# A recurrence's ScalarE and VectorE steps given an issue time 12 nominal microseconds ahead of their TensorE visit

## The chip, the cores and the metric

One Trainium2 chip, one of its cores. The metric is the device time of one execution in microseconds (us), as the median of several runs. TensorE, VectorE, ScalarE, GpSimd and SyncE each work through a list of instructions of their own, in order; semaphores hold an instruction until what it needs has been written.

In the rows of the profile PE is TensorE's matmuls, PEld its weight loads, DVE VectorE, ACT ScalarE, POOL GpSimd and SP SyncE.

## What is computed

A decoder layer with two kinds of heads side by side, on 1024 tokens of width 2048 in float32. One projection feeds an RWKV-7 mixer (16 heads of 64) and a sliding-window attention (16 query heads); a second projection brings both back. Cut to what matters here:

```python
h = rms_norm(x, norm_w)
z = h @ w_in                                   # 2048 x 6528
y_rwkv = rwkv7_mixer(z[..., :RWKV_COLS], ...)  # per head: a 64 x 64 state, one step per token
y_att  = swa_sink_mixer(z[..., RWKV_COLS:], ...)
return x + concatenate([y_rwkv, y_att]) @ w_out

def step(state, inp):                          # inside rwkv7_mixer
    r_t, w_t, k_t, v_t, kk_t, a_t = inp
    sa = einsum('bhvk,bhk->bhv', state, -kk_t)
    state = (state * w_t[:, :, None, :] + sa[..., None] * (kk_t * a_t)[:, :, None, :]
             + v_t[..., None] * k_t[:, :, None, :])
    return state, einsum('bhvk,bhk->bhv', state, r_t)
```

## The kernel before

**Tiling.** The 1024 tokens go through in two halves of 512. In each half there are eight units, u0 to u7 in the first and u8 to u15 in the second; a unit is a pair of RWKV heads together with a pair of attention heads. A unit computes six z tiles of 128 channels by 512 tokens. Each z tile is 48 matmuls of 128 x 512: the input and the weights are both split in a high and a low part, and three of the four products are taken (L346, L347 and L351). Each weight block is split by a ScalarE cast (L321) and a GpSimd subtraction (L322). After the eight units of each half comes the output projection (L798 to L800).

**The recurrence.** It doesn't go token by token. `rwkv_prep` rewrites 64 tokens (a chunk) as small matrices, and `rwkv_chain` carries the state through the 8 chunks c0 to c7 of a unit. Chunk c needs from its state `svu[:, :, c, :]`:

1. TensorE, L596: O = F x state, two small matmuls, one for each head.
2. ScalarE, L599: s0 = state scaled by the decay `pe`, two halves of 64 x 64; then L601 copies O over the state, again two halves.
3. TensorE, L603: ch = k x (that copy), and L604, which adds to O.
4. VectorE, L607: next state = ch x pe + s0, two halves; for c7 it goes to `scar`, the state kept for the other half of the tokens. The two halves are called the pair of the chunk here.

L596 of chunk c+1 needs the pair of chunk c. So a unit's chain is eight round trips TensorE, ScalarE, TensorE, VectorE, with no step of which another step of the same unit can run.

**What sets the order.** All work is written as generators that yield a nominal time; `run` takes the one with the earliest time, and `at(t)` gives what is then issued the priority `100000 + int(t * 1000)`. Every engine's list is made from these priorities and from what depends on what. A z matmul counts 0.32 nominal us, a z tile 15.36. The chain's chunk c is due at `tc0 = t0 + 91.5 + 5c`; its L603 and what follows at `tc0 + 2.5`.

What stands beside the chain of a unit in the lists, with its lines: on TensorE the z matmuls of the next unit, the attention's scores (L701, L702) and small products for the next unit's preparation (L398, L399, L573, L574); on VectorE the attention's score bias (L714), its maximum (L716, L718) and its normalising (L724, L725, L727) and the next unit's sigmoid, whose last step is a reciprocal of 128 x 512 (L410, L411); on ScalarE the copies of the scores out of PSUM (L706, L708), the exponentials (L723) and the weight casts (L321).

Of the kernel before, what the change touches and what calls it, by code (L numbers as in the profile page):

```python
# [64 lines left out]
def layer(tc, x, norm_w, w_in, w_out, mu_rwkv, w0, w2, a0, a2, k_k, k_a, r_k, lnx_w, lnx_b,  # L65
# [9 lines left out]
    def sb(shape, tag, bufs=1, dt=F32):  # L75
        return pool.tile(list(shape), dt, name=tag, tag=tag, bufs=bufs)
# [7 lines left out]
    def ps(tag, shape=(P, 512)):  # L84
        return psum.tile(list(shape), F32, name=tag, tag=tag, bufs={"z": 2, "m": 3, "o": 1, "ch": 1}[tag])
# [6 lines left out]
    def at(t):  # L92
        tc.cur_priority = 100000 + int(t * 1000)
# [490 lines left out]
    def rwkv_chain(t0, hf, p, S):  # L584
        yield t0 + 84
        F, bk, svu, pe = S["F"], S["bk"], S["svu"], S["pe"]
        for i, hr in enumerate(HR):
            G.tensor_copy(svu[hr, i, 0, :], scar[hr, p, :])

        O = ps("o", (P, NC, 2, 64))  # L590
        for c in range(NC):
            tc0 = t0 + 91.5 + c * 5
            yield tc0
            ch = chx[:, c % 2 * P:c % 2 * P + P].rearrange("p (i v) -> p i v", i=2)
            for i in range(2):
                PE.matmul(O[:, c, i, :], lhsT=F[c // 4][:, i, c % 4, :], rhs=svu[:, i, c, :], start=c % 4 == 0 and i == 0, stop=False, skip_group_check=True)  # L596
            s0 = sb([P, 64], "s0", 2)
            for i, hr in enumerate(HR):
                A.activation(s0[hr], svu[hr, i, c, :], AF.Copy, scale=pe[hr, c:c + 1])  # L599
            for i, hr in enumerate(HR):  # L600
                A.copy(svu[hr, i, c, :], O[hr, c, i, :])  # L601
            yield tc0 + 2.5
            PE.matmul(ch, lhsT=bk[:, c, :], rhs=svu[:, :, c, :], start=True, stop=True)  # L603
            PE.matmul(O[:, c], lhsT=Erb[:, c, :], rhs=svu[:, :, c, :], start=False, stop=c % 4 == 3, skip_group_check=True)  # L604
            for i, hr in enumerate(HR):
                dst = svu[hr, i, c + 1, :] if c < NC - 1 else scar[hr, p, :]
                V.scalar_tensor_tensor(dst, ch[hr, i, :], pe[hr, c:c + 1], s0[hr], ALU.mult, ALU.add)  # L607
        S["O"] = O
# [231 lines left out]
    def rwkv(t0, hf, p, S, *zs):  # L840
        yield from rwkv_prep(t0, hf, p, S, *zs)
        yield from rwkv_chain(t0, hf, p, S)
        yield from rwkv_post(t0, hf, p, S)
# [53 lines left out]
```

## Time and profile before

| what | value |
|---|---|
| median of 3 runs | 2040.49 us (2038.46 to 2042.29) |
| the profiled execution | 2035.18 us, of it span 2033.4 us |
| granted TensorE clock, mean | 0.988 |
| PE busy | 1956.4 us (96%), 13152 matmuls |
| PEld busy | 1588.8 us (78%) |
| DVE, ACT, POOL busy | 57%, 51%, 42% |

The span runs from the first to the last instruction. Matmul records overlap: a matmul of 128 x 512 has a record of about 0.40 us, and the next one starts 0.23 us after it. So a record's length is not what a matmul costs, and a stop of TensorE is read from the distance between two starts. A bracket at the end of a timeline row gives the idle time of that engine before the instruction and what released it. A wait can stand in the lists twice, once at the weight load (PEld) and once at the matmul (PE).

### The profile page before, as it was taken

What the parts mean: (1) busy time and instruction counts of PE and PEld (TensorE: products, weight loads), DVE (VectorE), ACT (ScalarE), POOL (GpSimd) and SP (SyncE); (2) the same over time, 40 slices, a digit from 0 to 9 for tenths busy, and PEclk for the clock granted to TensorE, in tenths of its full rate; (3) what the DMA queues carried; (4) which work ended last, traced back from release to release, by engine and by line L of the source; (5) the groups of instructions that cost most, each with busy time, mean ns of one, the idle gap of its engine ahead of it and who ended that gap; (6) DMA issues with size and microseconds to landing.
All of it is one profiled execution on the core that took longest, in us unless ns stands there. A gap on an engine that the chain in (4) does not pass through costs nothing.

```text
span 2033.4 us, 36474 instructions
## 1 busy us (share of the span) xinstructions
PE 1956.4 (96%) x13152; PEld 1588.8 (78%) x13152; DVE 1154.3 (57%) x2776; ACT 1038.9 (51%) x2563; POOL 855.4 (42%) x740
## 2 busy tenths in 40 slices
PE   7999999999999998899999999999999989999999
PEld 5777788777787776777777777787877779988887
DVE  6748485857667584775757575848585763011000
ACT  5445556565656464754546465655656552233221
POOL 4543534444453533153443435343433424444443
PEclk9999999999999998999999999999999989999999
DMA  7342423333232425133232424232332354454443
GB/s 178 89 99 56 99 66 89 81 76 84 75 96 64 104 71 138 52 88 74 64 93 57 101 59 100 65 94 66 84 82 76 82 173 135 146 172 157 136 138 115
DMA packets 412293, 197.01 MB, mean 97 GB/s; under 512 B 216941, under 2 KB 381136, under 8 KB 412112
## 3 DMA queue, kind: packets, MB, share of 16 engines
q1 hardware_dynamic: 371360, 181.90, 32.6%
q10 hardware_dynamic: 40000, 11.67, 2.4%
q0 software_dynamic: 752, 1.11, 0.5%
q8 instruction: 103, 1.69, 0.4%
q14 instruction: 78, 0.64, 0.1%
HBM read 173.51 MB, written 21.10 MB: 96 GB/s over the span
## 4 chain that ended last, share of the span: by engine, by line
PE 40%; DVE 8%; issue 3%; POOL 1%; ACT 1%; DMA 1%; ACTq 0%; SPq 0%; POOLq 0%; DVEq 0%
PE z L351 6%; PE z L346 6%; PE z L347 6%; PE z L798 2%; PE z L800 2%; PE z L799 2%; PE m L800 2%; PE m L798 2%; PE m L799 2%; POOL wl L322 1%; DVE ta L714 1%; PE o L800 1%; PE o L798 1%; PE o L799 1%; DVE t L411 1%
## 5 line engine op out<-in xcount | busy, mean ns | idle before, releaser
L322 POOL TENSOR_TENSOR wl<-wr,wh 128x512 fp32r<-128x512 f32 x536 | 704.4, 1318 | 952.2 <-ACT wh L321 506.7
L346 PE MATMUL z<-hh,wh 128*128 128x512 f32 x1632 | 661.4, 405 | 3.5 <-ACT hh L262 2.3
L347 PE MATMUL z<-hl,wh 128*128 128x512 f32 x1632 | 653.8, 401 | 0.0
L321 ACT CAST wh<-wr 128x512 fp32r<-128x512 f32 x536 | 329.8, 619 | 576.9 <-PE z L347 226.0
L351 PE MATMUL z<-hh,wl 128*128 128x512 f32 x1632 | 483.8, 406 | 0.0
L346 PEld LDWEIGHTS z<-hh,wh 128*128 128x128 f32 x1632 | 309.3, 190 | 71.1 <-ACT hh L262 4.0
L347 PEld LDWEIGHTS z<-hl,wh 128*128 128x128 f32 x1632 | 309.3, 190 | 62.0 <-DVE hl L263 0.2
L351 PEld LDWEIGHTS z<-hh,wl 128*128 128x128 f32 x1632 | 301.0, 190 | 65.1 <-issue 2.7
L354 DVE TENSOR_TENSOR z<-z,R 128x512 f32<-128x512 f32 x102 | 71.0, 696 | 111.5 <-PE z L351 109.3
L798 PE MATMUL z<-wh,hh 128*128 128x256 f32 (+1 forms) x352 | 112.2, 320 | 9.7 <-ACT hh L259 6.4
L599 ACT ACTIVATE s<-svu,pe 64x64 f32<-64x64 f32 x256 | 88.2, 344 | 51.7 <-DVE svu L607 47.9
L596 PEld LDWEIGHTS o<-svu,F 128*128 128x128 f32 x512 | 81.5, 189 | 38.8 <-DVE svu L607 30.9
L800 PE MATMUL z<-wh,hl 128*128 128x256 f32 (+1 forms) x352 | 111.2, 316 | 0.0
L799 PE MATMUL z<-wl,hh 128*128 128x256 f32 (+1 forms) x352 | 111.0, 316 | 0.0
L596 PE MATMUL o<-svu,F 128*128 128x64 f32 x512 | 85.9, 264 | 15.0 <-DVE svu L607 14.1
L479 DVE TENSOR_TENSOR pr<-X,ch 64x14 f32<-64x14 f32 (+6 forms) x224 | 42.1, 188 | 89.9 <-ACT ch L474 83.3
L806 DVE TENSOR_TENSOR ta<-z,ta 128x256 f32<-128x256 f32 (+1 forms) x22 | 10.0, 493 | 129.3 <-PE z L800 128.8
L798 PEld LDWEIGHTS z<-wh,hh 128*128 128x128 f32 x352 | 67.1, 191 | 15.1 <-ACT hh L259 6.8
L806 DVE TENSOR_TENSOR ta<-m,ta 128x512 f32<-128x512 f32 x9 | 6.1, 689 | 124.8 <-PE m L800 124.8
L607 DVE SCALAR_TENSOR_TENSOR svu<-ch,pe,s 64x64 f32<-64x64 f32 x224 | 62.9, 281 | 17.3 <-PE ch L603 11.1
L799 PEld LDWEIGHTS z<-wl,hh 128*128 128x128 f32 x352 | 67.2, 191 | 4.3
L800 PEld LDWEIGHTS z<-wh,hl 128*128 128x128 f32 x352 | 67.1, 191 | 4.4
(276 smaller groups left out, 3260.7 us busy)
## 6 DMA issues: line engine op xcount, KB each, us to landing
wr<-in_w_in SPq DMA_DIRECT2D x280, 256.0 KB, 2.9
wr<-in_w_in SPq DMA_DIRECT2D x256, 128.0 KB, 2.6
wr<-in_w_out SPq DMA_DIRECT2D x64, 256.0 KB, 2.9
wr<-in_w_out SPq DMA_DIRECT2D x128, 128.0 KB, 2.9
ta<-in_x SPq DMA_DIRECT2D x37, 256.0 KB, 5.0
zt<-yd SPq DMA_DIRECT2D x32, 256.0 KB, 3.5
out<-ta SPq DMA_DIRECT2D x24, 256.0 KB, 3.8
yd<-ta ACTq DMA_DIRECT2D x16, 256.0 KB, 2.0
```

The lines of the kernel that those rows point to most:

```text
L321: A.copy(hi[:], raw)
L322: G.tensor_tensor(lo[:], raw, hi[:].bitcast(F32), ALU.subtract)
L346: PE.matmul(z[:], lhsT=wh, rhs=hh[kk][:], start=(kk == 0), stop=False)
L347: PE.matmul(z[:], lhsT=wh, rhs=hl[kk][:], start=False, stop=False)
L351: PE.matmul(z[:], lhsT=lo[:, k * P:(k + 1) * P], rhs=hh[kk][:], start=False, stop=(kk == KT - 1))
L354: V.tensor_tensor(z[:], z[:], R[:], ALU.mult)
L596: PE.matmul(O[:, c, i, :], lhsT=F[c // 4][:, i, c % 4, :], rhs=svu[:, i, c, :], start=c % 4 == 0 and i == 0, stop=False, skip_group_check= ...
L599: A.activation(s0[hr], svu[hr, i, c, :], AF.Copy, scale=pe[hr, c:c + 1])
L607: V.scalar_tensor_tensor(dst, ch[hr, i, :], pe[hr, c:c + 1], s0[hr], ALU.mult, ALU.add)
L798: PE.matmul(o, lhsT=yh[k][:, ts], rhs=wh, start=k == 0 and tt % n == 0, stop=False, skip_group_check=True)
L799: PE.matmul(o, lhsT=yh[k][:, ts], rhs=wl, start=False, stop=False, skip_group_check=True)
L800: PE.matmul(o, lhsT=yl[k][:, ts], rhs=wh, start=False, stop=k == KT - 1 and tt % n == n - 1, skip_group_check=True)
```

## The change

In `rwkv_chain` two calls `at(tc0 - 12)` are put in: ahead of the loop of L599 (it holds for L601 too, up to the next `yield`), and, behind L603 and L604, ahead of the loop of L607. ScalarE's and VectorE's operations of chunk c thus get a priority of 12 nominal us before `tc0`, where they had `tc0` and `tc0 + 2.5`. TensorE's own chain instructions keep theirs. No instruction is added or removed on any engine.

```diff
             s0 = sb([P, 64], "s0", 2)
+            at(tc0 - 12)
             for i, hr in enumerate(HR):
                 A.activation(s0[hr], svu[hr, i, c, :], AF.Copy, scale=pe[hr, c:c + 1])
...
             PE.matmul(O[:, c], lhsT=Erb[:, c, :], rhs=svu[:, :, c, :], start=False, stop=c % 4 == 3, skip_group_check=True)
+            at(tc0 - 12)
             for i, hr in enumerate(HR):
                 dst = svu[hr, i, c + 1, :] if c < NC - 1 else scar[hr, p, :]
```

Lines from 598 on are one further down in the changed kernel, those from 605 on two: L599, L603 and L607 there read L600, L604 and L609, and L411 is L411 in both. In the pieces below a number behind a name is that of the buffer: `s0_12928` is the s0 of one chunk.

**VectorE, third unit of the second half (u10), around the reciprocal L411.** `s0_12928` belongs to the pair of c4, `s0_12973` to that of c5. Before:

```order
L716 TENSOR_REDUCE mx_13095<-ta_12796 128x4
L724 TENSOR_TENSOR sm_12865<-sm_12865,es_12863 128x4
L410 TENSOR_SCALAR t_12941<-m_12909 128x512
L725 RECIPROCAL sm_12865<-sm_12865 128x4
L718 TENSOR_SCALAR nm_13097<-mx_13095,snk_96 128x4
L727 TENSOR_SCALAR ta_12795<-ta_12795,sm_12865 128x128 x4
L411 RECIPROCAL t_12941<-t_12941 128x512
L724 TENSOR_TENSOR sm_13101<-sm_13101,es_13099 128x4
L607 SCALAR_TENSOR_TENSOR svu_12387<-ch_107,pe_11876,s0_12928 64x64
L725 RECIPROCAL sm_13101<-sm_13101 128x4
L607 SCALAR_TENSOR_TENSOR svu_12387<-ch_107,pe_11876,s0_12928 64x64
```

and now:

```order
L718 TENSOR_REDUCE mx_13095<-ta_12796 128x4
L609 SCALAR_TENSOR_TENSOR svu_12387<-ch_107,pe_11876,s0_12928 64x64 x2
L726 TENSOR_TENSOR sm_12865<-sm_12865,es_12863 128x4
L720 TENSOR_SCALAR nm_13097<-mx_13095,snk_96 128x4
L727 RECIPROCAL sm_12865<-sm_12865 128x4
L410 TENSOR_SCALAR t_12941<-m_12909 128x512
L729 TENSOR_SCALAR ta_12795<-ta_12795,sm_12865 128x128 x4
L411 RECIPROCAL t_12941<-t_12941 128x512
L609 SCALAR_TENSOR_TENSOR svu_12387<-ch_107,pe_11876,s0_12973 64x64 x2
L726 TENSOR_TENSOR sm_13101<-sm_13101,es_13099 128x4
```

The pair of c4 has moved from behind the reciprocal and a small sum to ahead of both, and its halves stand together; behind the reciprocal there is now the pair of c5. The same exchange is found in the steady units of both halves (u1 to u6, u10 to u14).

**TensorE, sixth unit of the first half (u5), the second chunk (c1), from its L596 to its L604.** `m_6948` and the like are score banks of the attention. Before:

```order
L596 MATMUL o_6741<-svu_6531,F_6118 128x64
L702 MATMUL m_6949<-kl1_115,Q_6595 128x128
L596 MATMUL o_6741<-svu_6531,F_6118 128x64
L701 MATMUL m_6948<-kh0_112,Q_6595 128x256
L702 MATMUL m_6948<-kl0_114,Q_6595 128x256
L701 MATMUL m_6949<-kh1_113,Q_6595 128x256
L702 MATMUL m_6949<-kl1_115,Q_6595 128x256
L603 MATMUL ch_107<-svu_6531,k4_6461 128x128
L604 MATMUL o_6741<-svu_6531,Erb_121 128x128
```

and now:

```order
L596 MATMUL o_6741<-svu_6531,F_6118 128x64 x2
L703 MATMUL m_6949<-kh1_113,Q_6595 128x128
L704 MATMUL m_6949<-kl1_115,Q_6595 128x128
L604 MATMUL ch_107<-svu_6531,k4_6461 128x128
L605 MATMUL o_6741<-svu_6531,Erb_121 128x128
```

Behind the second L596 four other matmuls stood ahead of L603 here, and now two. Further on in the same unit it goes the other way: between L596 and L603 of c5 and c6 stood 3 and 2 other matmuls, and there are now 6 and 8; between L604 of one chunk and L596 of the next stood 20 from c4 to c5, 2 from c5 to c6 and 8 from c6 to c7, and there are now 9, 10 and 8. In u10 these three were 20, 4 and 2, and are 9, 10 and 8.

**ScalarE, same unit, c1 and c2.** `s0_6871` belongs to c1, `s0_6908` to c2; L706 empties the score banks. Before:

```order
L599 ACTIVATE s0_6871<-svu_6531,pe_6022 64x64 x2
L601 COPY svu_6531<-o_6741 64x64 x2
L706 COPY ta_6939<-m_6948 128x128
L706 COPY ta_6940<-m_6949 128x128
L599 ACTIVATE s0_6908<-svu_6531,pe_6022 64x64 x2
```

and now:

```order
L600 ACTIVATE s0_6871<-svu_6531,pe_6022 64x64 x2
L602 COPY svu_6531<-o_6741 64x64 x2
L600 ACTIVATE s0_6908<-svu_6531,pe_6022 64x64
L708 COPY ta_6939<-m_6948 128x128
L600 ACTIVATE s0_6908<-svu_6531,pe_6022 64x64
L602 COPY svu_6531<-o_6741 64x64 x2
L708 COPY ta_6940<-m_6949 128x128
```

A scaling of c2, which needs the pair of c1, now stands ahead of copies that empty the banks into which L701 writes. On GpSimd one instruction stands one place earlier in some units, on SyncE 20 rows move; the other rows of TensorE keep their order but for some exchanges of L701 and L702.

## Rows read from the trace of the kernel before

**Rows 1.** The page's first part: busy us, share of the span, instructions.

```profile
PE 1956.4 (96%) x13152; PEld 1588.8 (78%) x13152; DVE 1154.3 (57%) x2776; ACT 1038.9 (51%) x2563; POOL 855.4 (42%) x740
```

**Rows 2.** Waits, whole span: engine, line, waited for: us, times, longest.

```profile
ACT s L599 <- DVE svu L607: 47.9, 62, 2.3
...
PEld o L596 <- DVE svu L607: 30.9, 44, 2.5
...
PEld ch L603 <- ACT svu L601: 27.5, 74, 0.8
...
PE o L596 <- DVE svu L607: 14.1, 19, 2.1
```

**Rows 3.** Busy us of each engine in 96 us stretches, instructions, clock, DMA share, GB/s.

```profile
584.00:680.00 96.00, 95.54 (x688) 76.73 (x688) 64.08 (x164) 55.85 (x145) 41.72 (x37) 1.00 0.32 82
...
1160.00:1256.00 96.00, 94.26 (x684) 75.72 (x683) 64.50 (x163) 55.38 (x143) 41.62 (x37) 1.00 0.32 82
```

**Rows 4.** Single lines: ns min/median/max of one, first and last start, forms.

```profile
L596 PE MATMUL o<-svu,F x512: 217/275/324, 140.5 to 1685.4; 128*128 128x64 f32 x171
...
L603 PE MATMUL ch<-svu,k x256: 270/275/378, 158.3 to 1686.8; 128*128 128x128 f32 x128
...
L607 DVE SCALAR_TENSOR_TENSOR svu<-ch,pe,s x224: 258/284/292, 159.2 to 1684.8; 64x64 f32<-64x64 f32 x112
```

**Rows 5.** Waits inside 626 to 660 us, the chain of u5.

```profile
PEld ch L603 <- ACT svu L601: 1.9, 5, 0.6
```

**Rows 6.** Timeline of TensorE in u5: start, us, line, operation, count, idle before.

```profile
642.20 0.38 PE L603 MATMUL ch<-svu,k 128*128 128x128 f32 x2
...
647.06 0.40 PE L346 MATMUL z<-hh,wh 128*128 128x512 f32 x1
647.47 0.43 PE L596 MATMUL o<-svu,F 128*128 128x64 f32 x2
```

**Rows 7.** Timeline of VectorE in the same stretch.

```profile
642.27 0.69 DVE L410 TENSOR_SCALAR t<-m 128x512 f32<-128x512 f32 x1
...
643.87 3.35 DVE L411 RECIPROCAL t<-t 128x512 f32<-128x512 f32 x1
647.13 0.10 DVE L724 TENSOR_TENSOR sm<-sm,es 128x4 f32<-128x4 f32 x1
647.15 0.27 DVE L607 SCALAR_TENSOR_TENSOR svu<-ch,pe,s 64x64 f32<-64x64 f32 x1
```

**Rows 8.** Timeline of TensorE in u10.

```profile
1200.13 0.40 PE L351 MATMUL z<-hh,wl 128*128 128x512 f32 x1
1201.61 0.44 PE L596 MATMUL o<-svu,F 128*128 128x64 f32 x2 [1.08 <-DVE svu L607]
```

**Rows 9.** Timeline of VectorE in u10.

```profile
1196.92 3.35 DVE L411 RECIPROCAL t<-t 128x512 f32<-128x512 f32 x1
1200.18 1.18 DVE L724 TENSOR_TENSOR sm<-sm,es 128x4 f32<-128x4 f32 x1
1201.29 0.27 DVE L607 SCALAR_TENSOR_TENSOR svu<-ch,pe,s 64x64 f32<-64x64 f32 x1
```

**Rows 10.** Timeline of GpSimd in u10.

```profile
1198.83 2.52 POOL L322 TENSOR_TENSOR wl<-wr,wh 128x512 fp32r<-128x512 f32 x2 [8.29 <-ACT wh L321]
```

**Rows 11.** Waits inside 1178 to 1216 us, the chain of u10.

```profile
PEld o L596 <- DVE svu L607: 3.0, 3, 1.5
```

**Rows 12.** Waits inside 1078 to 1118 us, the chain of u9.

```profile
PEld o L596 <- DVE svu L607: 4.1, 5, 2.5
```

**Rows 13.** Timeline of TensorE in u0 and in u7.

```profile
180.84 0.43 PE L596 MATMUL o<-svu,F 128*128 128x64 f32 x2 [1.37 <-DVE svu L607]
...
858.07 0.43 PE L596 MATMUL o<-svu,F 128*128 128x64 f32 x2 [1.35 <-DVE svu L607]
```

**Rows 14.** Timeline of VectorE in u0, ahead of that L596.

```profile
176.06 3.33 DVE L411 RECIPROCAL t<-t 128x512 f32<-128x512 f32 x1
...
180.50 0.29 DVE L607 SCALAR_TENSOR_TENSOR svu<-ch,pe,s 64x64 f32<-64x64 f32 x1
```

## The prediction, made before the changed kernel ran

> **What bounds the kernel now.** I began with the page's busy times: TensorE has matmuls on record for 96% of the span, no other engine comes near it [rows 1]. Then the busy times in stretches of about one unit: a stretch in the first half has 95.54 of 96 us, one in the second 94.26 [rows 3]. The rest of a unit that can be won is thus small, and the list of waits says where it lies: L596's weight loads wait 30.9 us in all for VectorE's L607, its matmuls 14.1 us more, and L603's weight loads 27.5 us for ScalarE's L601 [rows 2]. All three are the recurrence's round trip, which the change touches.
>
> How much of that is time? Records of matmuls overlap, so I worked from starts. For each of the 512 L596 and 256 L603 records [rows 4] I took the distance from the start of the matmul before, less the lower quartile of the distances between the same kinds of neighbours. That gives 45.2 us in all: 25.6 at L596 (waiting for VectorE) and 19.6 at L603 (waiting for ScalarE). By unit: 1.75 in each of u1 to u6; 3.4 in u10, u12 and u14; 2.64 in u11 and u13; 4.34, 3.80, 3.51, 4.56 and 3.01 in u0, u7, u8, u9 and u15. The windows agree in rank: u5's loads wait 1.9 us for ScalarE, u10's 3.0 and u9's 4.1 for VectorE [rows 5, 11, 12]. No change of order on ScalarE and VectorE can win more than the 45.2.
>
> On this the Trainium skill (Perfetto Trace Analysis, Identifying the Most-Contended Engine) says that matmul busy share is no good measure, because matmuls are pipelined, and that weight-load busy share should be taken. It is 78% here [rows 1]. The trace agrees so far as the matmul's own idle time shows only 14.1 us of L596's 25.6. Judged by that idle time alone, the sum below would shrink to about 14.1/25.6 of itself, some -7 us; by starts it is -12.5.
>
> The waits have one shape. In u10 TensorE starts a z matmul at 1200.13 and L596 only at 1201.61 [rows 8]: 1.48 us for a step of 0.23, with a switch between forms. On VectorE the reciprocal L411 ran from 1196.92 for 3.35 us, then a small sum L724 for 1.18, and only then came the awaited pair of c4, at 1201.29 [rows 9]. It had been ready for long, but stood behind both. In u5 it is the same, L411 at 643.87 and the pair at 647.15 [rows 7], but there the 20 matmuls between c4's L603 at 642.20 and L596 at 647.47 hid nearly all of it [rows 6]; 0.28 us is left. In u0 the pair's second half stood behind L411 at 176.06, and L596 shows 1.37 us of idle time at 180.84; u7 has 1.35 at 858.07 [rows 13, 14].
>
> **The change part by part.** Instructions: none is added or removed, and no DMA moves by more than its neighbours. What moves are 256 L599, 256 L601 and 256 L607 (224 of these write the next chunk's state, the other 32 the state kept). Each takes as long as before, an L607 258 to 292 ns [rows 4], so the busy sums stay and only waits change.
>
> VectorE, L607 earlier. (a) The pair of c4 leaves its place behind L411. Its wait at c5's L596 is by starts 2.62 us in u0, 1.62 in u7, 2.36 in u9, 1.35 in u10, u12 and u14, 0.26 in u11 and u13, 0.29 in u1 to u6: 12.9 in all, the largest item. With the pair ahead of L724, L410 and L411 it should be ready when c4's L603 is done, and 9 matmuls of 0.23 us follow that: 2.1 us of cover for a pair of 0.6 (two of 284 ns). I count it as gone. (b) The two halves stand together, so small rows no longer split them: c7's 0.42 in u10 to u14 goes, c4's 0.75 there falls to about 0.5. (c) Only the pair of c5 now stands behind L411. Stepping u5: c4's L603 at 642.20, its pair done about 643.2; L410 and its neighbours took 1.6 us from 642.27 to 643.87 [rows 7], and with L724 and L725 ahead of them about 2.0; so L411 runs from about 645.2 to 648.5, and c5's pair ends at about 649.0. c6's L596 is due after 9 + 6 + 10 matmuls (5.8 us) and the chain's own (about 1.2) from 642.5, at about 649.5. So 0.5 us of cover is left, nothing is lost in u1 to u6, and in the second half, where L724 can last 1.18 instead of 0.10 us [rows 7, 9], I allow 0.5 us in each of u10 to u14.
>
> ScalarE, L599 and L601 earlier. (d) L601's copy is what L603 waits for. At c6 its 0.33 in u1 to u6 falls to about 0.05, since 8 matmuls stand between L596 and L603 there and not 2. At c1, whose cover falls from four matmuls to two, the wait grows from 0.32 to 0.45; at c2 from 0.11 to 0.40; at c3 it falls from 0.46 to 0.30. (e) L599 of the next chunk, which waits for VectorE, now stands ahead of L706 and of a few casts. ScalarE waits so already, 62 times for 47.9 us [rows 2], and is idle half its time [rows 1]; the score banks it frees are needed a few matmuls later. I take this at nothing above (d), with an upper bound of 0.6 us, the longest of u5's five waits [rows 5], for each of c1 to c3, instead of 0.30 to 0.45. The lower bound is nothing, since a copy that is queued earlier can also end earlier.
>
> The sum. u1 to u6: -0.29 - 0.28 + 0.13 + 0.29 - 0.16 = -0.31 each, -1.9. u10, u12, u14: -1.35 - 0.25 - 0.42, against +0.12 at c1 to c3, +0.2 at c4's L603 and +0.5 at c6's L596: -1.2 each, -3.6. u11, u13: -0.26 - 0.25 - 0.42 - 0.18 + 0.82 = -0.3 each, -0.6. The irregular ones, where I take three quarters of the stall at c5's L596 and leave the rest: u0 -2.0, u9 -1.8, u7 -1.2; u8 and u15, whose waits lie elsewhere, -0.4 and -0.7 (one wait of 0.7 at c4 in u15). Together -6.1. All: -12.2, say -12.5 with the roundings. Against the profiled execution that is 2035.2 - 12.5 = 2022.7. That execution was 5.3 us under the median of the runs, which the sum doesn't touch: 2040.5 - 12.5 = 2028.
>
> One place hangs on what the 1.18 us of L724 is. GpSimd ran L322 from 1198.83 for 2.52 us, to 1201.35, so that L724 ended just as GpSimd did [rows 9, 10]; in u5 the same row took 0.10 [rows 7]. By the Trainium skill (SBUF — State Buffer, Who interferes with whom) a VectorE instruction with two SBUF inputs, as L724 has, contends with a GpSimd instruction that reads SBUF, and one with a single SBUF input, as L607 has beside PSUM, doesn't. The trace agrees: no L607 lasts over 292 ns. By that rule the hold stays with L724 and can reach the chain only through L411's start; if it belonged to the place behind L411 instead, the pair of c5 would inherit 1.08 us in u0, u10, u12 and u14, and the sum would be 4.3 us smaller.
>
> **The rivals.** *The waits change places, no measurable change* (0.2% is 4.1 us, about what a measurement of this kernel can tell). c1 to c3's L603 have fewer matmuls to hide behind, and ScalarE queues behind waiting L599s. At the bound of 0.6 for each of the three, eleven steady units give back 11 x 0.65 = 7 us; if the irregular units keep half of their stalls, 3 more: -2.5, 2038. For it: L603's waits are as large as L596's today [rows 2]. Against it: c5's stalls are single, long and behind one instruction that is no longer ahead of them.
>
> *Slower, by the reciprocal.* c5's pair now stands behind L411 in the eleven steady units and others like them, and L411 itself behind c4's pair, so that everything late in c4 is passed on to c5. My cover is 0.5 us. Each us of lateness past that is paid at c6's L596 in some 14 units. At 2 us late it is 14 x 1.5 = 21, in place of the 2.5 allowed: 2040.5 - 12.5 + 18.5 = 2046.5. It decides from about 1.6 us of lateness, where the sum is nil. For it: L411 is 3.35 us, longer than any cover but one. Against it: nothing in the row of work ahead of it adds up to 1.6 us more, unless L724 is held by GpSimd each time and something else with it.
>
> *The waits go altogether.* If all of L596's 25.6 us went and L603's stayed, 2015. Against it: a round trip has two eviction steps, and between chunks c1 to c3 there are only 2 to 4 small matmuls to hide one.
>
> *The change doesn't do what it says.* The engines' lists show that it does; left at 1%.
>
> **How the numbers follow.** My forecast, -6 to -19 us: 0.60. Places changed, -6 to +4: 0.19, of it 0.04 beyond 4.1 us faster. Slower by the reciprocal: 0.12, of it 0.01 within 4.1 us. All waits gone: 0.08. No effect: 0.01. Faster: 0.60 + 0.08 + 0.04 = 0.72; same: 0.15 + 0.01 + 0.01 = 0.17; slower 0.11. The range goes from 2019, a little under what the steps give if (c) costs nothing and (e) too, to 2041, which takes in most of the second case; left out are the slower case and most of the largest gain.
>
> **What would show it.** Right: in u0, u9 and u10 no stop at c5's L596, and the idle time of L596 for L607 falls from 45 us (weight loads and matmuls) to about half; L603's wait for L601 stays near 27 us or grows by a few; L411 starts about 1.3 us later beside the chain; no group's mean changes. A unit's period falls by 0.3 us in the first half and by about 1 in the second. Wrong: a stop at c6's L596 of more than 0.5 us in each unit (the reciprocal); L603's wait for L601 over 35 us (places changed); L701 waiting for L706, or z matmuls for their weights' casts, which no term of mine holds.

## The result and the profile after

The changed kernel took 2055.71 us (median of 5 runs, 2052.02 to 2057.38) beside 2038.46 us (2036.84 to 2042.29) for the kernel before on the same chip: 1.0084 times as long, interval 1.0071 to 1.0098. It is 17 us slower; 2028 with a range to 2041 had been forecast. The profiled execution took 2057.38 us, with a span of 2055.6 us against 2033.4 before; the granted clock is 0.988 in both. Lines below L599 keep their numbers; L599, L601, L603 and L604 are now L600, L602, L604 and L605, and every line from L607 on is two higher. What is said of a line in both kernels goes by its old number; rows show the new one.

The busy line of the page of after (busy us, share of the span, instructions):

```profile
PE 1961.9 (95%) x13152; PEld 1595.9 (78%) x13152; DVE 1171.6 (57%) x2776; ACT 1038.9 (51%) x2563; POOL 853.3 (42%) x740
```

Against [rows 1] VectorE is busy 17.3 us longer with the same 2776 instructions. ScalarE is where it was. The waits of after, whole span (engine, line, waited for: us, times, longest):

```profile
ACT s L600 <- DVE svu L609: 48.1, 58, 2.9
...
PEld ch L604 <- ACT svu L602: 31.0, 60, 1.6
...
PEld o L596 <- DVE svu L609: 23.9, 27, 2.8
PE o L596 <- DVE svu L609: 14.1, 18, 2.4
...
PE ch L604 <- ACT svu L602: 10.1, 19, 1.1
PEld m L745 <- DVE ta L736: 9.0, 13, 4.1
...
PE m L745 <- DVE ta L736: 5.8, 7, 3.6
```

Against [rows 2] L596's weight loads wait 7 us less, its matmuls as long as before, in fewer and longer stops. The wait of L603's matmul for L601's copy, 2.2 us before, is 10.1. The attention product's first matmul (old L743, new L745) waits longer for VectorE's L734, the softmax's masking product (new L736). Its two rows before were:

```profile
PEld m L743 <- DVE ta L734: 3.8, 2, 2.7
...
PE m L743 <- DVE ta L734: 3.1, 2, 2.2
```

By the prediction's own measure (distance between starts above the lower quartile of before), all of TensorE's stops grew from 153.1 to 174.5 us. That is 21.4 of the 22.2 us by which the spans differ, so the list is nearly whole. Which neighbours are put together moves the levels more than the differences: by the shapes of the two matmuls alone the same sum goes from 261.9 to 284.5, up 22.6. The largest parts (us, one execution each):

| TensorE's stop | before | after |
|---|---|---|
| L596 of c5, u0 to u14 | 12.9 | 1.5 |
| L596 of c7 in u0 and u9 | 0 | 6.9 |
| L603, all | 19.8 | 27.6 |
| L743 and L746, attention product | 28.3 | 39.4 |
| L798, output projection | 11.0 | 14.0 |

The first line is the forecast, and it came. For L603 the forecast had shifts that cancel; the other lines were in no term. What the table leaves out lies mostly at L596 of other chunks: c4 and c7 in u10 to u14, and c5 and c6 of u15, which show 0.43 and 0.34 us of idle time and none before. In u0 the stop that was at c5 [rows 13] stands two chunks later. Here are TensorE, VectorE and GpSimd in u0 of after (start, us, engine, line, operation, count, idle before):

```profile
184.06 0.38 PE L604 MATMUL ch<-svu,k 128*128 128x128 f32 x2
...
185.43 1.10 PE L351 MATMUL z<-hh,wl 128*128 128x512 f32 x4
188.88 0.43 PE L596 MATMUL o<-svu,F 128*128 128x64 f32 x2 [2.35 <-DVE svu L609]
```

```profile
179.41 0.60 DVE L609 SCALAR_TENSOR_TENSOR svu<-ch,pe,s 64x64 f32<-64x64 f32 x2
180.05 2.68 DVE L729 TENSOR_SCALAR ta<-ta,sm 128x128 f32<-128x128 f32 x4
...
183.78 2.93 DVE L729 TENSOR_SCALAR ta<-ta,sm 128x128 f32<-128x128 f32 x4
186.75 0.70 DVE L425 SCALAR_TENSOR_TENSOR m<-m,t 128x512 f32<-128x512 f32 x1
...
188.55 0.27 DVE L609 SCALAR_TENSOR_TENSOR svu<-ch,pe,s 64x64 f32<-64x64 f32 x1
```

```profile
179.72 2.54 POOL L322 TENSOR_TENSOR wl<-wr,wh 128x512 fp32r<-128x512 f32 x2 [7.14 <-ACT wh L321]
183.57 1.43 POOL L437 TENSOR_TENSOR Gt<-t 64x512 f32<-64x512 f32 x1 [1.32 <-DVE sm L727]
185.08 1.36 POOL L322 TENSOR_TENSOR wl<-wr,wh 128x512 fp32r<-128x512 f32 x1
```

The pair that c7's L596 awaits had its input at about 184.5 and came at 188.55. Ahead of it in VectorE's list stood two sets of L727 (the softmax's division, four `tensor_scalar` each) that took 2.68 and 2.93 us, and three operations of 0.7 us each behind the second. The same two sets in u0 of before:

```profile
174.35 0.88 DVE L727 TENSOR_SCALAR ta<-ta,sm 128x128 f32<-128x128 f32 x4
...
181.49 0.87 DVE L727 TENSOR_SCALAR ta<-ta,sm 128x128 f32<-128x128 f32 x4
```

That is 3.9 us more for the same work, next to c7's stop of 3.4 by starts. The long sets run just while GpSimd runs L322 or L437, the short ones don't. In the kernel before, that stretch of L322 began at 177.91, under the reciprocal L411 [rows 14], which is as long there as anywhere, and after L411's end it held L724 for 1.15 us; in after L411 had ended 0.45 us when it began. Over the whole span the line's own row says the same (ns of one: least, median, longest), first before, then after:

```profile
L727 DVE TENSOR_SCALAR ta<-ta,sm x128: 269/281/1316, 174.3 to 1679.2; 128x128 f32<-128x128 f32 x128
```

```profile
L729 DVE TENSOR_SCALAR ta<-ta,sm x128: 269/278/1397, 180.0 to 1699.5; 128x128 f32<-128x128 f32 x128
```

The median stays and the sum goes from 41.3 to 61.0 us. Counted one by one, 11 of the 128 lasted over 0.5 us before and 36 after. Every one of these 47 overlaps an L322 or L437 on GpSimd and ends 0.08 to 0.09 us after one of them has ended; of those that overlap neither (113 and 75), none lasts over 0.29.

### The profile page after: what moved, and what is told of

The parts are those of the page before. It is cut to its first block, busy times and chain, and to the rows that moved or that the text cites. A ratio compares the mean times of both kernels' runs of the same rounds, so it can differ in the third digit from the quotient of the medians.

```text
span 2055.6 us, 36477 instructions
## 1 busy us (share of the span) xinstructions
PE 1961.9 (95%) x13152; PEld 1595.9 (78%) x13152; DVE 1171.6 (57%) x2776; ACT 1038.9 (51%) x2563; POOL 853.3 (42%) x740
## 4 chain that ended last, share of the span: by engine, by line
PE 37%; DVE 9%; issue 3%; ACT 2%; POOL 1%; DMA 1%; ACTq 0%; SPq 0%; POOLq 0%; DVEq 0%
PE z L346 6%; PE z L351 6%; PE z L347 6%; PE m L802 2%; PE m L801 2%; PE z L800 2%; PE m L800 2%; PE z L802 2%; PE z L801 2%; POOL wl L322 1%; DVE ta L716 1%; PE o L802 1%; PE o L801 1%; PE o L800 1%; DVE ta L729 1%
## 5 line engine op out<-in xcount | busy, mean ns | idle before, releaser
L322 POOL TENSOR_TENSOR wl<-wr,wh 128x512 fp32r<-128x512 f32 x536 | 702.7, 1315 | 981.4 <-ACT wh L321 500.1
L351 PE MATMUL z<-hh,wl 128*128 128x512 f32 x1632 | 476.5, 403 | 0.0
L600 ACT ACTIVATE s<-svu,pe 64x64 f32<-64x64 f32 x256 | 88.1, 344 | 51.9 <-DVE svu L609 48.1
L596 PEld LDWEIGHTS o<-svu,F 128*128 128x128 f32 x512 | 78.4, 189 | 32.5 <-DVE svu L609 23.9
L596 PE MATMUL o<-svu,F 128*128 128x64 f32 x512 | 82.6, 269 | 14.4 <-DVE svu L609 14.1
L800 PEld LDWEIGHTS z<-wh,hh 128*128 128x128 f32 x352 | 68.0, 193 | 17.6 <-ACT hh L259 7.3
L609 DVE SCALAR_TENSOR_TENSOR svu<-ch,pe,s 64x64 f32<-64x64 f32 x224 | 62.0, 277 | 18.8 <-PE ch L604 13.6
L604 PEld LDWEIGHTS ch<-svu,k 128*128 128x128 f32 x256 | 42.6, 188 | 38.0 <-ACT svu L602 31.0
```

Of the source, the lines that this page charges most:

```text
L322: G.tensor_tensor(lo[:], raw, hi[:].bitcast(F32), ALU.subtract)
L351: PE.matmul(z[:], lhsT=lo[:, k * P:(k + 1) * P], rhs=hh[kk][:], start=False, stop=(kk == KT - 1))
L800: PE.matmul(o, lhsT=yh[k][:, ts], rhs=wh, start=k == 0 and tt % n == 0, stop=False, skip_group_check=True)
```

## The experiments

Each pair below puts one edit into the kernel before and into the changed one; the second median less the first is what the change costs in that setting. A single median is uncertain by some 2 to 4 us, and stops are read in one execution each; those of e1, e2, e12 and e17 took 4 to 7 us less than their medians. "By starts" is the measure of the table above.

**The two halves of the change, and c4 alone.** `e1` has only the second `at`, `e2` only the first, `e5` both for one chunk.

```
e1:          yield tc0 + 2.5
             ...
+            at(tc0 - 12)
             for i, hr in enumerate(HR):
                 dst = svu[hr, i, c + 1, :] if c < NC - 1 else scar[hr, p, :]
e2:          s0 = sb([P, 64], "s0", 2)
+            at(tc0 - 12)
             for i, hr in enumerate(HR):
                 A.activation(s0[hr], svu[hr, i, c, :], AF.Copy, scale=pe[hr, c:c + 1])
e5, at both places:
+            if c == 4:
+                at(tc0 - 12)
```

> Only the second of the two calls, the one ahead of L607 on VectorE. Theory A (the loss comes from VectorE: the order behind the reciprocal has changed, the normalising L727 now runs beside GpSimd's L322 and is held, and the pair of c6 in u0 and u9 and the attention's product at L743 and L746 wait for it): most of the 17 us stays, 2049 to 2056 us, L727's busy time near 60 us. Theory B (the loss comes from ScalarE: L601 stands in the queue behind exponentials that wait for VectorE, and L603 waits for it): little is left, 2036 to 2042 us.

> Only the first of the two calls, the one ahead of L599 and L601 on ScalarE. Theory A: no loss, 2035 to 2042 us, L727's busy time near 41 us. Theory B: 8 us and more of loss, 2046 to 2056 us, L603's waits for L601 up by 8 us or more.

> Both calls, but only for chunk c4, the one whose pair stood behind the reciprocal; the other seven chunks keep their priorities. Theory A (each pair moved ahead of the reciprocal hands its wait on: VectorE's maximum L716 and L718 behind it come later, so ScalarE's exponentials do, and L601 of c5 stands behind these): c5's L596 no longer waits (-13 us), but its L603 waits 1 to 1.5 us in each of 11 steady units (+11 to +16), in all 2033 to 2044 us. Theory B (moving c4's pair is the gain that was forecast, and the loss comes from the other chunks): 2023 to 2030 us.

Measured: e1 2048.94 (ratio 1.0052, 1.0032 to 1.0071), e2 2053.59 (1.0069, 1.0045 to 1.0094), e5 2041.28 (1.0013, 0.9999 to 1.0027). Either half alone is slower. For e2 one theory had expected no loss and the other more waiting at L603; it lost 16.5 us against 2037.1 before, with L603's stops no larger and c5's L596 at about twice its stop. In e1 the L603 of c5 stops 1.46 us in u5, more than in the whole change. e2 left the pairs of L607 after L411 and put a set of L727 between; u5 of e2, VectorE, GpSimd and TensorE:

```profile
646.85 3.32 DVE L411 RECIPROCAL t<-t 128x512 f32<-128x512 f32 x1
650.09 2.38 DVE L728 TENSOR_SCALAR ta<-ta,sm 128x128 f32<-128x128 f32 x4
652.47 0.27 DVE L608 SCALAR_TENSOR_TENSOR svu<-ch,pe,s 64x64 f32<-64x64 f32 x1
```

```profile
649.48 2.52 POOL L322 TENSOR_TENSOR wl<-wr,wh 128x512 fp32r<-128x512 f32 x2 [6.54 <-ACT wh L321]
```

```profile
652.79 0.43 PE L596 MATMUL o<-svu,F 128*128 128x64 f32 x2 [1.59 <-DVE svu L608]
```

So a set that had taken 0.88 us ahead of L411 took 2.38 beside L322, and the pair behind it was late. In e5, c5's stop goes and c6's takes its place (0.1 to 0.58 us by starts in u5, none to 1.57 in u11), while c5's L603 stops 0.29 in u5 and not the 1 to 1.5 expected. There the waits did change places: freeing the pair of c4 alone wins nothing.

**L727 cut to one column.** L727 keeps its place in the queue, but divides only the first column of each tile, so the softmax isn't normalized.

```
-                V.tensor_scalar(L3[:, b, :], L3[:, b, :], sm[:, b:b + 1], None, ALU.mult)
+                V.tensor_scalar(L3[:, b, 0:1], L3[:, b, 0:1], sm[:, b:b + 1], None, ALU.mult)
```

> The kernel before with the normalising L727 on one column of each 128 (the other 127 columns stay unnormalised): 128 instructions as before, but short ones. It is the base for the next run. Theories A and B alike: 2033 to 2040 us, since TensorE waited for L727 or what is behind it only in a few places.

> The changed kernel with the same cut of L727 (127 of each 128 columns stay unnormalised). Theory A: without long L727s there is nothing to hold, so against the kernel before with the same cut the loss falls from 17 to 8 us or less, and the stops of 3.4 us at c7's L596 in u0 and u9 go. Theory B: the loss against that stays at 14 us or more.

Measured: e3 2019.36 (0.9911, 0.989 to 0.9932), e4 2031.63 (0.997, 0.9957 to 0.9983). L727 now lasts at most 0.22 us each, 26.4 and 25.9 us in all. The kernel before gains 18 us by it, where 4 at the most had been expected. The change's loss at L743 is gone (16.5 us in both, against 15.9 and 23.2 without the cut), and c7 in u0 and u9 falls from 6.9 to 1.6. Yet the change still costs 12.3 us, so L727's length is not the whole cause: 8.7 of it are at L603 (17.6 to 26.3), the rest is spread over L798 and smaller stops.

**L727 on another engine.** The full computation; L727 on ScalarE (`e6` before, `e8` after, `e7` e5's kernel) or on GpSimd (`e15`, `e16`).

```
-                V.tensor_scalar(L3[:, b, :], L3[:, b, :], sm[:, b:b + 1], None, ALU.mult)
e6, e7, e8:
+                A.activation(L3[:, b, :], L3[:, b, :], AF.Copy, scale=sm[:, b:b + 1])
e15, e16:
+                G.tensor_scalar(L3[:, b, :], L3[:, b, :], sm[:, b:b + 1], None, ALU.mult)
```

> The kernel before with the normalising L727 as 256 operations... of ScalarE instead of VectorE (128 in all, the same columns, same result). Theory A (L727's long holds beside GpSimd are what delays the chain and the attention's tail): most of the 18 us that the cut to one column won is kept, 2020 to 2030 us. Rival (ScalarE's 0.39 us for each, 3 us more in a unit, come ahead of L599 and L601): 2036 us or more.

> The calls for c4 alone, and L727 on ScalarE. Theory A: c5's L603 stands behind still more of ScalarE's work, so slower than the run with L727 on ScalarE alone by 5 us or more. Theory B: faster than that by 5 to 13 us.

> The changed kernel with L727 on ScalarE. With the cut to one column the change still cost 12 us. Theory A (that rest is L603 waiting for L601 in ScalarE's queue): against the kernel before with L727 on ScalarE the change costs 12 us or more, and L603's waits are the largest term. Rival (the rest is VectorE's own order): the cost stays at 8 us or less.

> The kernel before with the normalising L727 on GpSimd (same result). Theory C: VectorE is rid of 41 us and of the holds by its own L727; if GpSimd needs 0.3 to 0.5 us for each of 128, it has the room (42% busy): 2020 to 2033 us. Against it: GpSimd's list is in order too, and L322 behind an L727 that waits for the softmax brings the weights late: 2040 us or more.

> The changed kernel with L727 on GpSimd. Theory C: as with L727 on ScalarE, the change costs 3 us or less or even gains up to 8 against the run above, since the gain at c5's L596 is no longer eaten. Rival D: it costs 12 us or more.

Measured: e6 2042.74 (1.0008, 0.9997 to 1.002), e7 2042.13 (1.0013, 1.0 to 1.0025), e8 2042.49 (1.0008, 0.9995 to 1.0021), e15 2046.59 (1.0031, 1.002 to 1.0043), e16 2043.95 (1.002, 1.0008 to 1.0033). The change costs -0.3 and -2.6 us, and e7 is no different from e6, where one theory had it slower and the other faster. By starts L596 falls from 29.9 (e6) to 18.1 us (e8), and L743 stays (16.4, 16.5). But little of that fall is the forecast's: c5 had only some 6 us left in e6, and c6 in u1 to u6 gives as much. L603 and smaller stops give it all back. No version is faster than the kernel before.

**The reciprocal.** In `e9` and `e10` L411 is an operation of 0.42 us whose result isn't the reciprocal. In `e12` (before) ScalarE computes it.

```
-        V.reciprocal(n2[:], n2[:])
e9, e10:
+        V.tensor_scalar(n2[:], n2[:], 1e-24, 1e-9, ALU.mult, ALU.add)
e12:
+        A.activation(n2[:], n2[:], AF.Ln)
+        A.activation(n2[:], n2[:], AF.Exp, scale=-1.0)
```

> The kernel before with the reciprocal L411 replaced by a multiply and add of the same tile (0.7 us in place of 3.35; the key norms are then wrong). It prices the length of L411. Theory A (the length of L411 is what c5's L596 pays for): L596's waits fall from 26 us to 12 or less and the time to 2012 to 2027 us. Rival (something else would hold VectorE there in any case): 2030 us or more.

> The changed kernel with the same short operation in place of L411. Theory A (the change only hands the reciprocal's 3.35 us on to later pairs and to the attention's tail): without it the change costs less than half of its 17 us, so within 8 us of the kernel before with the short operation. Rival (the loss lies in ScalarE's queue and in L727, and has nothing to do with the reciprocal): 12 us or more above it.

> The kernel before with the reciprocal taken as exp(-ln x) by two operations of ScalarE instead of L411 on VectorE. If the length of L411 on VectorE is what the chain pays for, and ScalarE has the room (51% busy): 2020 to 2032 us, faster than both kernels. If the two operations (1.2 us and what switching between functions costs) come ahead of L599 and L601 or of L723: 2036 us or more.

Measured: e9 2055.32 (1.0091, 1.0067 to 1.0116), e10 2050.59 (1.0051, 1.0034 to 1.0067), e12 2045.47 (1.0034, 1.0022 to 1.0045). Taking some 2.9 us of VectorE's work out of each unit makes the kernel before 17 us slower. u5 of e9, VectorE, GpSimd and TensorE:

```profile
655.14 0.59 DVE L607 SCALAR_TENSOR_TENSOR svu<-ch,pe,s 64x64 f32<-64x64 f32 x2
...
658.38 2.92 DVE L727 TENSOR_SCALAR ta<-ta,sm 128x128 f32<-128x128 f32 x4
...
661.72 0.60 DVE L607 SCALAR_TENSOR_TENSOR svu<-ch,pe,s 64x64 f32<-64x64 f32 x2
```

```profile
658.44 1.37 POOL L322 TENSOR_TENSOR wl<-wr,wh 128x512 fp32r<-128x512 f32 x1 [0.36 <-ACT wh L321]
659.94 1.27 POOL L437 TENSOR_TENSOR Gt<-t 64x512 f32<-64x512 f32 x1
```

```profile
662.05 0.76 PE L596 MATMUL o<-svu,F 128*128 128x64 f32 x4 [2.17 <-DVE svu L607]
```

The set of L727 now meets L322 and L437 and takes 2.92 us where it took 1.17, and c6's L596 stops some 2.4 us longer in each of u1 to u6, which is most of the 17. So the long instruction had been a shelter: what ran on GpSimd beside it did not lengthen it. In e12 the two activations stand ahead of L601's copy on ScalarE, each in u5 behind a load of its function table of 1.28 us, and c5's L603 stops 1.26 us in u1 to u6, where it stopped 0.10:

```profile
647.80 1.28 ACT L411 ACT_TABLE_LOAD   x1
649.10 0.63 ACT L411 ACTIVATE t<-t 128x512 f32<-128x512 f32 x1
```

**ScalarE's exponentials.** In `e11` (after) the four exponentials of each unit's second head cover one column of each tile, so half of the softmax is left out.

```
+                if i == 0:
                     A.activation(L3[:, b, :], L3[:, b, :], AF.Exp, bias=nm[:, b:b + 1], accum_out=sm[:, b:b + 1])
+                else:
+                    A.activation(L3[:, b, 0:1], L3[:, b, 0:1], AF.Exp, scale=0.0, accum_out=sm[:, b:b + 1])
```

> The changed kernel with the exponentials L723 of each unit's second attention head cut to one column and a constant (that head's softmax is left out). They stand ahead of c5's L601 in ScalarE's queue. Theory A: c5's L603 stops waiting (0.79 us in u1 to u6, 1.1 to 1.4 in u0, u7 and u9), 2043 to 2050 us. Rival (c5's L603 waits for something else): no change at c5, 2052 to 2058 us.

Measured: 2049.0 (1.005, 1.0035 to 1.0065); c5's L603 stops 1.02 us in u5, not less than the 0.79 of after. Other work took the place ahead of the copy, as ScalarE's rows in u5 of e11 show:

```profile
651.74 0.63 ACT L419 ACTIVATE t<-sig 128x512 f32<-128x512 f32 x1
652.27 0.60 ACT L321 CAST wh<-wr 128x512 fp32r<-128x512 f32 x1
652.90 0.44 ACT L602 COPY svu<-o 64x64 f32<-64x64 f32 x2
```

The time lies in the range that theory A gave, but not by its way: c5's stop stayed, and the stops at c7 in u0 and u9 and at L798 fell instead. So it isn't the length of these exponentials that counts for c5's L603, but what stands ahead of the copy in the queue.

**GpSimd's subtraction.** In `e13` and `e14` L322 fills the weights' low part with zeros and reads nothing (the low parts are left out of the product). In `e17` and `e18` VectorE does L322, with the full computation.

```
-        G.tensor_tensor(lo[:], raw, hi[:].bitcast(F32), ALU.subtract)
e13, e14:
+        G.memset(lo[:].bitcast(F32), 0.0)
e17, e18:
+        V.tensor_tensor(lo[:], raw, hi[:].bitcast(F32), ALU.subtract)
```

> The kernel before with GpSimd's subtraction L322 for the weights replaced by writing zeros (the weights' low parts are left out). GpSimd then reads nothing there, and the order on the other engines is the same but for a few places. Theory C (L727 is held by GpSimd's reads): L727's busy time falls from 41 to about 36 us and L724's from 10 to about 5; the time falls by 5 to 15 us, to 2023 to 2033. Rival D (L727 is late for another reason): busy times as before, 2033 to 2043.

> The changed kernel with the same replacement. Theory C: L727 falls from 61 us to about 36, the stops of 3.4 us at c7's L596 in u0 and u9 shrink to 1 us or less, the attention's product at L743 and L746 waits no longer than before, and the change costs 8 us or less against the run above (what is left is L603). Rival D: the cost stays at 14 us or more.

> The kernel before with the weights' subtraction L322 on VectorE instead of GpSimd (same result). VectorE gets 536 operations of about 0.7 us (375 us) and loses its holds (some 70 us), so it is busy for about 75% of the span. If the holds are what costs: 1990 to 2025 us. Against it: chain and low parts now share one list, and pairs stand behind subtractions, or L351 behind late low parts: 2040 to 2080 us.

> The changed kernel with L322 on VectorE. Theory C (the change's loss is made by GpSimd's reads): the change costs nothing against the run above, from 3 us more to 10 us less, since early pairs now also pass subtractions. Rival D: it costs 12 us or more.

Measured: e13 1983.63 (0.9725, 0.9709 to 0.9742), e14 1980.54 (0.9711, 0.9693 to 0.9728), e17 2070.5 (1.0151, 1.013 to 1.0172), e18 2069.14 (1.0146, 1.0129 to 1.0163). The change costs -3.1 and -1.4 us. The pages of e13 and of e14:

```profile
PE 1937.0 (98%) x13152; PEld 1582.1 (80%) x13152; DVE 1082.5 (55%) x2776; ACT 1036.6 (52%) x2563; POOL 433.4 (22%) x740
```

```profile
PE 1934.2 (98%) x13152; PEld 1586.9 (80%) x13152; DVE 1084.8 (55%) x2776; ACT 1038.3 (52%) x2563; POOL 436.1 (22%) x740
```

e13 lies 39 us below both ranges expected. VectorE, on which nothing was edited, is busy 72 us less in e13 than in [rows 1], though L727 gives only 3.7 of it. The waits of L596 in e13, then in e14:

```profile
PEld o L596 <- DVE svu L607: 7.3, 21, 1.0
...
PE o L596 <- DVE svu L607: 1.2, 3, 0.8
```

```profile
PEld o L596 <- DVE svu L609: 2.6, 8, 0.6
...
PE o L596 <- DVE svu L609: 0.5, 1, 0.5
```

A unit of the first half stops 1.60 us in e13 and 1.32 in e14. That this gain of 0.28 is near the forecast's 0.31 is chance: it lies at L603 of c3, c5 and c6, and c5's L596 had no stop left in e13 that could go. There the pair of c4 stands in its old place behind L411, as in u10 of e13:

```profile
1159.13 3.35 DVE L411 RECIPROCAL t<-t 128x512 f32<-128x512 f32 x1
1162.39 0.10 DVE L724 TENSOR_TENSOR sm<-sm,es 128x4 f32<-128x4 f32 x1
1162.40 0.27 DVE L607 SCALAR_TENSOR_TENSOR svu<-ch,pe,s 64x64 f32<-64x64 f32 x1
```

L724 takes 0.10 us and not 1.18 [rows 9], and c5's L596 stops some 0.4 us in all 16 units together, where it had stopped 12.9.

These two runs do more than stop the reads, though: the fill is shorter than the subtraction (0.53 us for 1.29), so the weights are ready sooner. And the fill still holds L727. In e14 L727 takes 48.0 us, not the 36 expected, and 25 of the 128 last over 0.5 us, each beside an L437 or a fill:

```profile
1253.78 0.82 DVE L729 TENSOR_SCALAR ta<-ta,sm 128x128 f32<-128x128 f32 x2
```

```profile
1253.98 0.54 POOL L322 MEMSET wl<- 128x512 f32 x1
```

No L724 of e13 or e14 lasts over 0.17 us, though 22 of the 64 overlap L437 or a fill. So GpSimd's reads are what held L724, but L727 is held by an instruction that reads nothing too. In e17 and e18, with no L322 on GpSimd, no L727, L718 or L724 lasts over 0.29 us. In e18 the stops at L743 grow by 10.8 us with no L322 on GpSimd (the two executions read differ by 8 us, where the medians differ by -1.4), so a VectorE that is late for another reason costs there too.

## Why the prediction was wrong

**(a) held in its number.** c5's stop went, 12.9 to 1.5 us in u0 to u14, where the sum had left a quarter of it in u0, u7 and u9, 1.6 us. The pair had stood behind two instructions, and the second weighed as much as the first: in e13, with L411 as long as ever but L724 not held, c5 hardly stops, and in u10 L724's hold was 1.08 of the 1.35 us. So part of what the change freed was itself a hold by GpSimd.

**The premise under all the terms failed:** "Each takes as long as before, an L607 258 to 292 ns [rows 4], so the busy sums stay and only waits change." True of L607 (median 284 ns in both, none over 293 in after), false of what it changes places with. L727 alone grew by 19.7 us. With it the change loses 6.9 us at c7 in u0 and u9 and 7.3 at L743. That this loss is L727's hold is shown by e3 with e4 and by e6 with e8: a short L727 or one on ScalarE takes most (e4) or all (e8) of the u0 and u9 stop away and all of L743's growth; e9 makes a stop of the same kind in the kernel before. L746's growth of 3.8 us goes only in part with it.

The sign was in rows that I had read: L724 took 1.18 us in u10, up to the end of L322, and 0.10 in u5 [rows 7, 9, 10]. I put it down to an instruction with two SBUF inputs and asked only where L724 and L607 would land. In u0 and u5 of before, L727's sets took 0.87 and 1.17 us; 11 instructions of that line had been held already. The rule I cited has a second half: the Trainium skill (SBUF — State Buffer, Who interferes with whom) counts `tensor_scalar` among the operations that can take both SBUF ports, and says that whichever of VectorE and GpSimd comes second waits for the other's whole instruction. The trace agrees: every L727 over 0.5 us overlaps L322 or L437. It also agrees that L607, with one input in PSUM, isn't held: 60 of them overlap GpSimd's two lines in after, none over 0.293 us. The reciprocal isn't among the operations that the Trainium skill names there: in the kernel before all 16 of L411 overlap L322 or L437, and none lasts over 3.35 us.

**(d) was mis-sized.** The forecast for L603 was small shifts that nearly cancel; measured +7.8 us. In u1 to u6 c1 has 0.57 (forecast 0.45), c2 0.34 (0.40), c3 0.18 (0.30), c6 none (0.05), all near. The miss is c5, 0.10 to 0.79, which no term held, and 1.1 to 1.4 in u0, u7 and u9. Follow it back in u5 of after, ScalarE, VectorE, GpSimd and TensorE:

```profile
647.65 0.30 ACT L722 ACTIVATE es<-nm,snk 128x4 f32<-128x4 f32 x1 [0.54 <-DVE nm L720]
...
651.84 0.39 ACT L725 ACTIVATE ta<-ta,nm 128x128 f32<-128x128 f32 x1
...
653.12 0.44 ACT L602 COPY svu<-o 64x64 f32<-64x64 f32 x2
```

```profile
646.55 1.07 DVE L720 TENSOR_SCALAR nm<-mx,snk 128x4 f32<-128x4 f32 x1
```

```profile
646.30 1.29 POOL L322 TENSOR_TENSOR wl<-wr,wh 128x512 fp32r<-128x512 f32 x1
```

```profile
653.61 0.49 PE L604 MATMUL ch<-svu,k 128*128 128x128 f32 x2 [0.52 <-ACT svu L602]
```

A `tensor_scalar` of four columns (L718, new L720) took 1.07 us to the end of L322. ScalarE waited for it, its exponentials came late, and L601's copy stood behind them. L718 lasts over 0.5 us 3 times of 32 before and 8 times after. In e14, where 1 does, c5's L603 doesn't stop in u1 to u6 at all; in e4, e8, e10 and e16, with 8 again, it stops 0.75 to 0.82. In e18, where none does, it stops 0.28 in each of u1 to u6, and e17 as much on the mean. So this is the same premise failing a second time, with ScalarE's order as the carrier. It also answers most of what e4 left at L603: the cut of L727 doesn't touch L718.

**(c) and the rival by the reciprocal.** The cover of c6's L596 held: 0.16 us in u1 to u6, none in u10 to u14 (0.5 allowed). The slower outcome therefore came by a road that my slower rival didn't name; with the reciprocal shortened (e10 against e9) the change even costs -4.7 us, but that setting has held sets of its own in before, so it says little of L411's price.

**(b) failed.** In u10 to u14 c7's 0.42 became 0.67, and c4's 0.75 became 1.21, where 0 and 0.5 were forecast. **(e)** L701, which waits for the banks that L706 frees, costs nothing (1.9 us by starts before, 0.1 after), and ScalarE's wait for L607 is 48.1 us beside 47.9 [rows 2].

**Units.** The chain of u10 to u14 fell from 3.4 and 2.64 to 2.9 us, so with -1.2 and -0.3 forecast the odd units lost; a unit of u1 to u6 went from 1.75 to about 2.25, where -0.31 was forecast, almost all of it c5's L603.

**What stays open.** The settings in which the change costs nothing (e6 with e8, e13 with e14, e15 with e16, e17 with e18) each shift other stops too: e8's first half has a new 1.15 us at c7 and its second half none. They show that the 17 us hang on which VectorE work meets GpSimd's, and don't price each hold. e13, e14, e17 and e18 also change when the weights are ready. Of the 12.3 us in e4 the new 0.7 at c7 in u1 to u6 and the growth at L798 have no cause shown; nor has what stays of L746's growth. That an order with the pairs early and the `tensor_scalar` sets clear of GpSimd's work would win the 12.5 us wasn't tried.

## What to carry to other kernels

Before you move work ahead in an in-order queue, list what it changes places with, and look up what the neighbouring engine runs at the new times: an instruction whose longest is four times its median, as L727's, L718's and L724's were here, may be held by something, and then its duration belongs to its place, not to it. A long instruction on a side engine may be the cover under which another engine's work runs free; shortening or passing it can cost more than it gives. A wait that is freed at one step of a round trip is a gain only if the next step's cover is longer than what was freed (e5: c5's stop became c6's).

## What the runs showed of the hardware

- A 128x128 `tensor_scalar` on VectorE takes 0.28 us and up to 1.40 beside a GpSimd subtraction of 128x512; even a four-column one (0.23 us) took 1.07. Beside a GpSimd fill, which reads nothing, the 128x128 one took 0.52 to 0.69 (e14); a small `tensor_tensor` isn't held by the fill. The 128x512 reciprocal takes 3.35 us, beside GpSimd's subtraction or not.
- With GpSimd's subtraction replaced by a fill, VectorE's busy time falls by 72 us of 1154 (e13), on the same 2776 instructions.
- Less work on VectorE made the kernel slower: 17 us for a reciprocal shortened to an eighth (e9).
- With the reciprocal as two activations ScalarE loads its function tables 33 times, 1.28 us each, where it had loaded them once (e12).
